# A row-sum kernel: the program's last wait is moved from SyncE to GpSimd

## The chip, the cores and the metric

The kernel runs on one core of a Trainium2 chip. The core has five engines with an instruction stream each: TensorE, VectorE (called DVE in the profile), ScalarE (ACT), GpSimd (POOL) and SyncE (SP). They meet through numbered semaphores alone. The time is that of the device in microseconds (us), from run to run; the profile shows one execution of the program, and its span runs from the program's first instruction to its last.

## The reference

```python
def setup_inputs():
    batch, seq, dim = 32, 512, 1024
    return {"x": np.random.randn(batch, seq, dim).astype(np.float32)}

def reference(x):
    return np.sum(x, axis=-1).astype(np.float32)
```

16,384 rows of 1,024 numbers in float32 are each summed: 67.11 MB are read and 0.07 MB written.

## The kernel before

The rows are laid over 128 partitions, 128 rows to each, in three blocks of 32, 48 and 48 (`BLOCKS`). Each block is cut into groups of 16 rows per partition (`G`), eight groups in all, and three buffers `xt` take them in turn. All transfers, loads and stores, are issued by SyncE, in the order of the list `loads` (L149); a load into a buffer that is in use waits until DVE has done with it. The first row of the first group has a load of its own, so that DVE can start early, and the last group comes in pieces: rows 0 to 8, 9 to 12 and 13 to 14 (`CUTS`), and then the last row in two parts, into the tile `tail`.

DVE sums most rows (L63), and by pairs the row before the end and the last one (L81). ScalarE takes seven rows of the second last group and about half of the last group's first pieces (L74). Sums are collected in `res`. GpSimd has no work in the kernel; it sets four constants at the program's start and takes part in the barriers there (L208, L169).

When the last group's pieces have arrived, SyncE issues three early stores (L155), for all results that are already there; they count up the semaphores `early0` to `early2`. When DVE and ScalarE have done their last instruction, it issues the last store (L159), of the last group's 16 results per partition, which counts up the semaphore `store` by 16 when it has landed. Then the program ends with three steps on SyncE: it waits for the three early stores (L161, recorded on L162), clears all semaphores of the kernel but `store` (L163), and waits for the last store and takes `store` back to zero (L164). The semaphores have to be zero again when the program ends, as the next execution starts from them.

Two of the loads are moved by hand ahead of the starting barrier (`EARLY`), which is why SyncE's first issue opens the span.

Of the kernel before, what the change touches and what calls it, by code (L numbers as in the profile page):

```python
# [19 lines left out]
def row_sums(nc, x: bass.AP, out: bass.AP):  # L20
# [33 lines left out]
    sems = {n: nc.alloc_semaphore(n) for n in names}  # L54
# [106 lines left out]
    for k in range(len(stores)):  # L161
        nc.sync.wait_ge(sems[f"early{k}"], 16)  # L162
    nc.sync.sem_clear(range(numbers[0], sems["store"].num))  # L163
    nc.sync.wait_ge(sems["store"], 16).then_inc(sems["store"], -16)  # L164


def kernel(tc: tile.TileContext, x: bass.AP, out: bass.AP):
    tc.close()
    tc.compile()  # L169
    nc = tc.nc  # L170
    row_sums(nc, x, out)

    sp = mybir.EngineType.SP
    fn = nc.m.functions[0]
    entry, body = None, None
    for blk in fn.blocks:
        ops = [i for i in blk.instructions if i.engine == sp]
        if entry is None:  # L180
            entry = blk
        elif any(i.opcode == "DMACopy" for i in ops):
            body = blk
            break
    code = list(body.instructions)
    loads = [i for i in code if i.engine == sp and i.opcode == "DMACopy"][:EARLY]
    for load in loads:
        assert not load.sync_info.on_wait
        code.remove(load)
    body.instructions = code  # L190
    code = list(entry.instructions)
    at = next(k for k, i in enumerate(code) if i.engine == sp and i.opcode == "Drain")
    code[at:at] = loads
    entry.instructions = code
# [29 lines left out]
```

## Time and profile before

| what | us |
|---|---|
| median of 3 runs | 160.84 |
| the three runs | 160.83, 160.84, 161.23 |
| the profiled execution, its time | 160.73 |
| the profiled execution, its span | 159.4 |
| last store, from issue (157.95) to landing | 1.4 |

The span is shorter than the time, as it holds the program's own instructions alone: what the system runs ahead of them and behind them is outside of it. In the profile, a row such as "L164 SPq EVENT_SEMAPHORE" gives a line of the kernel, the engine whose instruction queue it is (SPq is SyncE's, POOLq GpSimd's), the kind, and then the shortest, median and longest duration in ns and the start of the first and last. The duration of a semaphore instruction begins when what it waits for is there; the wait itself stands in the list of waits. In that list a line gives who waited for whom, the sum in us, how often, and the longest.

Beside instructions, the trace has a record of every change of a semaphore, with its number and time. The kernel's own semaphores have the numbers 99 to 113 (`store` is 113); the starting barriers use 96 and 97. Times of such records are given here in us from the start of the span.

### The profile page before, as it was taken

Reading aid. Unit: us, or ns where it says so; the run is one execution under the profiler, and the core shown is the slowest. Engines: PE = TensorE matmul, PEld = TensorE weight load, DVE = VectorE, ACT = ScalarE, POOL = GpSimd, SP = SyncE. Lnnn points to the kernel's source line nnn. Section 1 sums busy time; section 2 is a strip of 40 time slices with the busy share of each in tenths; the row PEclk is TensorE's granted clock in tenths of the full one; section 3 lists DMA queues with packets and bytes.
Section 4 is the critical chain, followed back from the end, with each engine's and each line's share of the span. In section 5 each row is a group of like instructions: output and inputs, shape, how many; then the busy total and the mean of one; then the engine's idle time right before and its main releaser. Section 6 shows DMA issues by size and latency. Waiting matters only on the chain.

```text
span 159.4 us, 110 instructions
## 1 busy us (share of the span) xinstructions
DVE 121.5 (76%) x17; ACT 17.2 (11%) x31; POOL 0.2 (0%) x4
## 2 busy tenths in 40 slices
DVE  1100059994799968999499994999949999499685
ACT  3000000000000000000000000000000000494694
POOL 0000000000000000000000000000000000000000
DMA  9988996996997989969969969969979799699994
GB/s 378 493 370 370 493 526 263 526 526 263 526 477 312 526 378 411 526 263 526 526 263 526 526 263 526 526 263 526 460 329 526 312 477 526 296 444 444 387 400 151
DMA packets 2448, 67.18 MB, mean 421 GB/s; under 512 B 784, under 2 KB 912, under 8 KB 1168
## 3 DMA queue, kind: packets, MB, share of 16 engines
q1 hardware_dynamic: 2448, 67.18, 98.2%
HBM read 67.11 MB, written 0.07 MB: 421 GB/s over the span
## 4 chain that ended last, share of the span: by engine, by line
DMA 75%; DVE 22%; SPq 1%; issue 0%
DMA xt<-in_x_dram 50%; DMA tail<-in_x_dram 25%; DVE res L63 22%; SPq L149 1%; DVE pairs L81 0%; DVE res L81 0%
## 5 line engine op out<-in xcount | busy, mean ns | idle before, releaser
L63 DVE TENSOR_REDUCE res<-xt 128x16 f32<-128x16384 f32 (+5 forms) x10 | 119.9, 11994 | 34.1 <-DMA xt<-in_x_dram 34.1
L74 ACT ACTIVATE xt<-xt 128x1024 f32<-128x1024 f32 x15 | 15.6, 1043 | 138.3 <-DMA xt<-in_x_dram 138.3
L74 ACT ACTIVATION_READ_ACCUMULATOR xt<-xt 128x1 f32 x15 | 2.8, 187 | 0.0
L107 DVE MEMSET tail<- 128x1 f32 x1 | 0.1, 59 | 2.0 <-PEq L169 2.0
L74 ACT ACT_TABLE_LOAD x1 | 1.3, 1283 | 1.9 <-PEq L169 1.9
L81 DVE CUSTOM_DVE_ANT_0 pairs<-tail 128x272 f32<-128x272 f32 (+1 forms) x2 | 0.9, 428 | 0.1
L81 DVE CUSTOM_DVE_ANT_0 pairs<-xt 128x512 f32<-128x512 f32 x1 | 0.7, 693 | 0.2 <-DMA xt<-in_x_dram 0.2
L81 DVE DVE_READ_ACCUMULATOR2_ANT res<- 128x1 f32 x2 | 0.2, 82 | 0.0
L208 POOL MEMSET const-bfloat16-1.0<- 128x1 bf16 x1 | 0.1, 102 | 0.0
L208 POOL MEMSET const-uint8-127<- 128x1 uint8 x1 | 0.1, 101 | 0.0
L208 POOL MEMSET const-float32-0.0<- 128x1 f32 x1 | 0.1, 99 | 0.2 <-issue 0.2
L208 POOL MEMSET const-float32-1.0<- 128x1 f32 x1 | 0.1, 98 | 0.0
L81 DVE DVE_READ_ACCUMULATOR2_ANT tail<- 128x1 f32 x1 | 0.1, 82 | 0.0
## 6 DMA issues: line engine op xcount, KB each, us to landing
xt<-in_x_dram SPq DMA_DIRECT2D x1, 7680.0 KB, 21.2
xt<-in_x_dram SPq DMA_DIRECT2D x1, 4608.0 KB, 32.6
xt<-in_x_dram SPq DMA_DIRECT2D x1, 2048.0 KB, 37.0
xt<-in_x_dram SPq DMA_DIRECT2D x1, 1024.0 KB, 39.0
xt<-in_x_dram SPq DMA_DIRECT2D x1, 512.0 KB, 3.5
tail<-in_x_dram SPq DMA_DIRECT2D x1, 272.0 KB, 39.2
tail<-in_x_dram SPq DMA_DIRECT2D x1, 240.0 KB, 39.3
xt<-in_x_dram SPq DMA_DIRECT2D x6, 40.8
```

The source lines that it names most:

```text
L63: nc.vector.tensor_reduce(out=res[:, c : c + n], in_=t[:, j * D : (j + n) * D].rearrange("p (j d) -> p j d", d=D), axis=X, op=ADD,).then_i ...
L74: nc.scalar.activation(out=v, in_=v, func=COPY, accum_out=res[:, c + i : c + i + 1]).then_inc(act, 1)
L81: nc.vector.tensor_tensor_reduce(out=pairs[:, 0 : h - a], in0=t[:, a:h], in1=t[:, h:b], scale=1.0, scalar=0.0, op0=ADD, op1=ADD, accum_out ...
L107: nc.vector.memset(tail[:, CUT + 15 : CUT + 16], 0.0).then_inc(vec, 1)
L149: nc.sync.dma_start(out=dst, in_=src).then_inc(s, 16)
L208: nc = _bacc.Bacc("TRN2", target_bir_lowering=False, num_devices=1)
```

## The change

One word on the program's last line: the wait for `store`, and the decrement that goes with it, are given to GpSimd's instruction stream. SyncE's program ends with the clear of the other semaphores.

```diff
     for k in range(len(stores)):
         nc.sync.wait_ge(sems[f"early{k}"], 16)
     nc.sync.sem_clear(range(numbers[0], sems["store"].num))
-    nc.sync.wait_ge(sems["store"], 16).then_inc(sems["store"], -16)
+    nc.gpsimd.wait_ge(sems["store"], 16).then_inc(sems["store"], -16)
```

All other instructions stand on the same engines in the same order.

## The prediction

> **What bounds the kernel now.** I read the page's head and chain first, then SyncE's waits in the last ten microseconds, then the rows of the lines that end the program, and last the semaphore records of the trace. The page first:
>
> ```profile
> span 159.4 us, 110 instructions
> DVE 121.5 (76%) x17; ACT 17.2 (11%) x31; POOL 0.2 (0%) x4
> ...
> q1 hardware_dynamic: 2448, 67.18, 98.2%
> ...
> DMA 75%; DVE 22%; SPq 1%; issue 0%
> ```
>
> The DMA queue is busy for 98.2% of the span, so the body is bound by reading 67.11 MB, and GpSimd does 0.2 us of work in all. Nothing in the body touches the edited line: what counts is what comes after the last data. The chain of waits ends there:
>
> ```profile
> 118.14 39.32 DMA tail<-in_x_dram
> 157.46 0.05 issue
> 157.51 0.41 DVE pairs L81
> 157.92 0.01 DVE res L81
> ```
>
> After 157.93 us only SyncE is at work. Its issues in the timeline, its waits from 150 us on, and the rows of L163 and L164:
>
> ```profile
> 156.22 1.30 SPq L155 DMA_DIRECT2D out_dram<-res  x3
> 157.95 0.33 SPq L159 DMA_DIRECT2D out_dram<-res  x1
> ```
>
> ```profile
> SPq L164 <- SPq L164: 0.6, 1, 0.6
> SPq L162 <- DMA out_dram<-res: 0.4, 1, 0.4
> ```
>
> ```profile
> L163 SPq EVENT_SEMAPHORE_RANGE_CLEAR  x1: 51/51/51, 158.7 to 158.7; - x1
> ```
>
> ```profile
> L164 SPq EVENT_SEMAPHORE  x1: 17/17/17, 159.4 to 159.4; - x1
> ```
>
> The last store is issued at 157.953 us and its sixteenth landing is recorded at 159.361. SyncE has waited for the early stores by 158.660, cleared the other semaphores from 158.729 to 158.780, and then sat 0.6 us in the wait of L164, which starts at 159.378 and ends at 159.395. That is the end of the span.
>
> The profiled execution took 160.73 us against a span of 159.40, so 1.33 us lie around the program. Part of that can be seen in the semaphore records. Semaphore 2, which no line of the kernel uses, is counted up in rounds of nine, once before the program (-0.375 to -0.004 us) and twice after. The round at the end has its updates at 2.127, 157.489, 157.527, 158.076, 159.539, 159.582, 159.620, 159.654 and 159.701 us. Four of the first five follow the end of an engine's work: TensorE's (its barrier row of L169 ends at 1.893 us), ScalarE's (157.376), DVE's (157.925), SyncE's (159.395). That leaves the third, 38 ns behind ScalarE's, for GpSimd. I read it as a chain TensorE, ScalarE, GpSimd, DVE, SyncE and back; the records name no engine, so the order is inferred. After 159.701 the remaining semaphores are written to (until 160.265), and a last round ends at 160.847. So SyncE's end at 159.395 pushes all this, and whoever ends last sets it.
>
> **The change, part by part.** Removed: one wait on SyncE, 17 ns of execution and a 17 ns reaction (159.361 to 159.378). SyncE then ends with its clear at 158.780, 0.615 us earlier. Its four stores and their issues stay where they are, and so do all loads, so the landing at 159.361 stays.
>
> Added: one wait on GpSimd. It stands at the end of GpSimd's program: no instruction of the kernel is behind it, no engine waits for one, and no transfer of GpSimd's queue exists. All that is behind it is GpSimd's place in the chain on semaphore 2. GpSimd sits in it from about 1.9 us to the landing, which costs nothing (ScalarE sits 134.7 us in a wait likewise). Its price has rows:
>
> ```profile
> L169 POOLq EVENT_SEMAPHORE  x4: 17/17/17, 1.4 to 1.8; - x4
> L169 POOLq DRAIN  x2: 34/38/41, 1.2 to 1.5; - x2
> ```
>
> GpSimd's semaphore instruction takes 17 ns like SyncE's. Its reaction is 25 ns: in two of the program's starting barriers the last arrival is recorded at 1.358 and 1.685 us and GpSimd's wait begins at 1.382 and 1.710. So GpSimd ends at 159.361 + 0.025 + 0.017 = 159.403, 8 ns after SyncE in the kernel before. The span becomes 159.40 again.
>
> [...]
>
> Next, GpSimd's step from its last instruction to its update of semaphore 2. No row shows this for GpSimd, because it was always waiting for its predecessor. The others: ScalarE 113 ns (157.376 to 157.489), SyncE 144 (159.395 to 159.539), DVE 151 (157.925 to 158.076), TensorE 234 (1.893 to 2.127). Bounds 113 and 234; I take SyncE's 144, since both end in the same instruction with the same 17 ns.
>
> Then the rest of the chain. When SyncE came last, four updates remained: 159.539 to 159.701, 162 ns. When GpSimd comes last, six remain: GpSimd to DVE to SyncE and all the way back. The records hold a round in which the third came last, before the program: -2.709, -2.665, -2.641, -2.528, -2.490, -2.455, -2.405, which is 304 ns. The round from -0.375 gives 298 for the same stretch. From below, if SyncE's turn took 43 ns as at 159.582 rather than 113: about 230 ns. From above, if GpSimd is not third but first, with 322 ns from its last row (1.805) to 2.127 and a whole round of 371 ns behind it.
>
> Sum: 159.403 + 0.144 + 0.304 = 159.851 in place of 159.701, that is +0.150 us. Low end: 159.403 + 0.113 + 0.230 = 159.746, +0.045. High end: 159.403 + 0.322 + 0.371 = 160.096, +0.395. A gain is excluded inside this reading, since GpSimd's landing, reaction and chain each are no shorter than SyncE's but for the 31 ns between ScalarE's step and SyncE's.
>
> What is late next: the writes to the semaphores and the last round, which begin behind 159.701 and move with it. Against the profiled execution this is 160.73 + 0.15 = 160.88; the median of the three runs, 160.84, lies 0.11 above that execution, so I forecast 160.99, rounded to 161.0. The body cannot hide any of it, nor add to it.
>
> **The rivals.** A difference of under 0.3%, 0.48 us, is what a measurement of this kernel hardly tells from none; the three runs alone span 0.40 us.
>
> Slower: GpSimd has work of its own behind the program, before it enters the chain. In the kernel before this would have been hidden, because GpSimd is done at 1.8 us and is called at 157.5. In the long round before the program GpSimd's place (-2.709) came 627 ns behind ScalarE's (-3.336), where the other hops are 24 to 50 ns and one 113, so something there kept it back. Its drains of 34 to 41 ns, against 7 to 10 of the others, point the same way, but weakly. Against it: its share of the semaphore writes (numbers 105 to 155, 159.760 to 160.060) is as quick as its neighbours'. If 627 ns come on top of the 144, the end is 159.403 + 0.771 + 0.304 = 160.478, +0.78, and the time 161.62. It decides from the point where GpSimd's step is longer than 144 + 330 = 474 ns, which is where the whole loss passes 0.48 us.
>
> Faster: the time is closed by SyncE's own stream, or by what it does for the queue that it alone issues on, and not by the last engine. SyncE ends 0.615 us earlier, so 160.84 - 0.62 = 160.22. Against it: its semaphore writes (numbers from 207 on) start at 159.664, behind the chain's turn, so SyncE cannot run ahead of the others.
>
> No change at all: what follows the span is not in the time, or is of fixed length. Then only the 8 ns count, 160.85. For it: I do not see where the 160.73 begin and end. Against it: 1.33 us more than the span must come from somewhere, and the records hold 1.45 us behind it.
>
> That the change does not do what it says I can leave aside: the wait stands at the end of GpSimd's program, and the landings it waits for are the same sixteen.
>
> **How the numbers follow.** The forecast 0.56; GpSimd's own work 0.30; no change at all 0.06; SyncE closes the time 0.08. The forecast has more than half because each of its terms has a row, and the second has 0.30 because the one step without a row is the one that it speaks of. Faster by over 0.3% is the last, 0.08; within 0.3% the first and third, 0.62; slower 0.30. The range is 160.7 to 161.65: from a little under no change, for the scatter of the runs, up to the slower rival's 161.62; it leaves out the faster one's 0.08 and some scatter. The forecast's own range is 160.84 + 0.045 to 160.84 + 0.395, 160.89 to 161.24.
>
> By Runtime: NRT & Kernel Launch of the Trainium skill (section The ~15µs preamble/postamble breakdown) a hop of such a barrier over five engines takes 44 ns, eight in all. Six hops would be 264 ns where the rows have 304, and the sum 160.95; the measured round decides.
>
> **What would show it.** The span of the changed kernel should be 159.4, with SyncE's last row the clear of L163 and a GpSimd row of 17 ns on L164 some 25 ns behind the last landing. On semaphore 2, the third update should stand some 0.14 us behind that row, and six more should follow within 0.30 us, so that the round ends about 0.49 us behind the landing's last record instead of 0.34. A third update over 0.47 us behind the GpSimd row proves the slower rival; a round that ends by itself as before, with a shorter time, the faster one. I am wrong too if the landing itself moves, since I left the body untouched.

## The result and the profile after

| | before | after |
|---|---|---|
| median of 8 runs, us | 160.74 | 161.31 |
| the runs, us | 160.62 to 161.23 | 161.01 to 161.61 |
| profiled execution, time, us | 160.73 | 161.42 |
| profiled execution, span, us | 159.4 | 159.5 |

The ratio is 1.0032, with a 95% interval from 1.0022 to 1.0042: about half a microsecond lost. Run again later, the changed kernel gave 1.0035 (1.0021 to 1.0050). The page of the changed kernel, its head, its queue and its chain:

```profile
span 159.5 us, 110 instructions
...
DVE 121.5 (76%) x17; ACT 17.2 (11%) x31; POOL 0.2 (0%) x4
...
q1 hardware_dynamic: 2448, 67.18, 98.0%
...
DMA 75%; DVE 22%; SPq 1%; issue 0%
```

The body is as it was. SyncE's waits from 150 us on, and the rows of L163 and L164 after the change:

```profile
SPq L159 <- DVE res L81: 0.4, 1, 0.4
SPq L162 <- DMA out_dram<-res: 0.4, 1, 0.4
```

```profile
L163 SPq EVENT_SEMAPHORE_RANGE_CLEAR  x1: 51/51/51, 158.9 to 158.9; - x1
```

```profile
L164 POOLq EVENT_SEMAPHORE  x1: 17/17/17, 159.5 to 159.5; - x1
```

SyncE no longer waits for the last store, its program ends with the clear of L163, and the wait of L164 is GpSimd's, of the same 17 ns. In the span, then, next to nothing is lost (8 ns, as the table shows). The loss lies behind it, in the records of semaphore 2. The table has the end of both profiled executions, in us, and in ns the parts in between:

```
                                        before      after
last landing of the store              159.361    159.496
the last engine's program ends         159.395    159.538     34 ->  42
its update of semaphore 2              159.539    160.099    144 -> 561
last update of that round              159.701    160.383    162 -> 284
last update of the last round          160.847    161.531   1146 -> 1148
landing to end of the first round                            340 -> 887
```

Read from the top: the landing itself came 135 ns later in this execution. The last store was issued that much later already, at 158.09 us in place of 157.95, because the loads ended later:

```profile
158.09 0.33 SPq L159 DMA_DIRECT2D out_dram<-res  x1
```

This is scatter of the loads, not the edit: a second execution of the changed kernel has the landing at 159.450 us, and two of the kernels below with the last wait on SyncE have it at 159.205 and 159.521. From the landing to the end of the round it is 547 ns more: 8 for the reaction, 417 more in the step from the last engine's last instruction to its update, 122 for the rest of the chain. What follows is the same length. 135 + 547 + 2 make 0.684 us, and the two profiled times differ by 0.69.

### The profile page after: what moved, and what is told of

Its sections match the earlier page's. It is cut to its first block, busy times and chain, and to the rows that moved or that the text cites. A ratio compares the mean times of both kernels' runs of the same rounds, so it can differ in the third digit from the quotient of the medians.

```text
span 159.5 us, 110 instructions
## 1 busy us (share of the span) xinstructions
DVE 121.5 (76%) x17; ACT 17.2 (11%) x31; POOL 0.2 (0%) x4
## 4 chain that ended last, share of the span: by engine, by line
DMA 75%; DVE 22%; SPq 1%; issue 0%
DMA xt<-in_x_dram 50%; DMA tail<-in_x_dram 25%; DVE res L63 22%; SPq L149 1%; DVE pairs L81 0%; DVE res L81 0%
```

## Experiments

**GpSimd ends early, SyncE keeps the last wait** (`gp_early`). The first early store's semaphore is moved behind those of the other two in the list of names (the first two lines of the edit), so that SyncE's clear stops ahead of it.

```diff
-    names += ["tail1", "vec", "act", "early0", "early1", "early2", "store"]
+    names += ["tail1", "vec", "act", "early1", "early2", "early0", "store"]
     ...
-    for k in range(len(stores)):
+    for k in (1, 2):
         nc.sync.wait_ge(sems[f"early{k}"], 16)
-    nc.sync.sem_clear(range(numbers[0], sems["store"].num))
+    nc.sync.sem_clear(range(numbers[0], sems["early0"].num))
+    nc.gpsimd.wait_ge(sems["early0"], 16).then_inc(sems["early0"], -16)
     nc.sync.wait_ge(sems["store"], 16).then_inc(sems["store"], -16)
```

> SyncE keeps the last wait; GpSimd waits for the first early store instead and takes its semaphore back. Theory A (GpSimd has a step of its own of about 0.56 us between its last instruction and its update of semaphore 2, whatever it waited for): GpSimd ends about 157.7 us, its update follows about 0.56 us later, near 158.25, where it stood at 157.53 before; SyncE's update at about 159.54 still comes later, so the time is that of before, 160.74 within 0.1%. Theory B (the step is that dear only for the engine that ends last, for instance because the others are already waiting): the update stands about 0.15 us behind GpSimd's last instruction, time 160.74 as well.

Measured: 0.9991 (0.9978 to 1.0004). GpSimd's row, in the view of its line:

```profile
L164 POOLq EVENT_SEMAPHORE  x1: 17/17/17, 157.9 to 157.9; - x1
```

It ends at 157.896, and the third update of semaphore 2 comes at 158.457: 561 ns, to the nanosecond the step of the changed kernel, though SyncE's program ends 1.66 us later (159.555). From the last landing (159.521) to the end of the round it is 340 ns, as in the kernel before. So the step does not come from ending last; it is there all the time, and in the kernel before it was hidden, because GpSimd had nothing to do from 1.8 us on. Theory B falls.

**The last wait on each of the other engines** (`last_act`, `last_dve`, `last_pe`). One word is changed on the last line, here for ScalarE:

```diff
-    nc.sync.wait_ge(sems["store"], 16).then_inc(sems["store"], -16)
+    nc.scalar.wait_ge(sems["store"], 16).then_inc(sems["store"], -16)
```

> ScalarE holds the last wait. Theory A (the loss belongs to GpSimd): reaction 22 ns, 17 ns, step 113 ns, then 336 ns of chain: 0.49 us from the last landing record to the end of the round in place of 0.34, so +0.15 us, ratio 1.001. Theory C (any engine other than SyncE pays about 0.42 us more than its hops): 0.90 us, +0.57 us, ratio 1.0035.

> VectorE holds the last wait. Theory A: reaction 28 ns, 21 ns, step 151 ns, then 254 ns of chain: 0.45 us from the last landing record to the end of the round, +0.11 us, ratio 1.0007. Theory C: 0.87 us, +0.53 us, ratio 1.0033.

> TensorE, which heads the chain, holds the last wait. Theory A: reaction 30 ns, 51 ns, step 234 ns, then the whole round of 371 ns: 0.69 us from the last landing record to the end of the round, +0.35 us, ratio 1.002. Theory C: 1.1 us, +0.77 us, ratio 1.0048.

Measured: 1.0015 (1.0006 to 1.0024), 1.0012 (1.0003 to 1.0021) and 1.0026 (1.0013 to 1.0039). The rows of the last line, first the kernel with ScalarE, then with VectorE, then with TensorE:

```profile
L164 ACTq EVENT_SEMAPHORE  x1: 17/17/17, 159.4 to 159.4; - x1
```

```profile
L164 DVEq EVENT_SEMAPHORE  x1: 21/21/21, 159.3 to 159.3; - x1
```

```profile
L164 PEldq EVENT_SEMAPHORE  x1: 51/51/51, 159.2 to 159.2; - x1
```

From the records, in ns (the sum of a row is the way from the last landing to the end of the round):

```
last engine   landing to its end   step   rest of the chain    sum
TensorE               79            279          357           715
ScalarE               38            149          324           511
GpSimd                42            561          284           887
VectorE               49            182          240           471
SyncE                 34            144          162           340
```

The rest of the chain falls from row to row by 33 to 78 ns. That shows the order, which the prediction had only inferred: TensorE, ScalarE, GpSimd, VectorE, SyncE, and back. The records show it directly too: with the wait on TensorE no update stands ahead of the wait's end, with ScalarE one, GpSimd two, VectorE three and SyncE four, and the others follow one after another. The steps of TensorE, ScalarE and VectorE are 31 to 45 ns longer here than the 234, 113 and 151 ns in the prediction, where another instruction was their last; so a step is not one number for an engine. All three results lie by theory A (0.51, 0.47 and 0.71 us where 0.49, 0.45 and 0.69 were expected) and far from theory C. GpSimd is the only engine with a step over 0.3 us, so its loss is more than its place in the chain.

**More instructions on GpSimd behind the wait** (`gp_pad`).

```diff
-    nc.gpsimd.wait_ge(sems["store"], 16).then_inc(sems["store"], -16)
+    nc.gpsimd.wait_ge(sems["store"], 16).then_inc(sems["store"], 1)
+    for i in range(17, 24):
+        nc.gpsimd.wait_ge(sems["store"], i).then_inc(sems["store"], 1)
+    nc.gpsimd.wait_ge(sems["store"], 24).then_inc(sems["store"], -24)
```

> As the changed kernel, but the wait is followed on GpSimd by eight more semaphore instructions that have nothing to wait for (about 78 ns each by the starting barriers, some 0.62 us in all). Theory A (fixed work behind the program's end): the step from GpSimd's last instruction to its update of semaphore 2 stays 0.56 us, and the time grows by the eight instructions, to about 161.9, ratio to before 1.007. Theory D (the step is code or a state that is fetched once GpSimd wakes, and that goes on beside whatever it executes): the eight instructions hide most of it, the step falls below 0.3 us, and the time is about that of the changed kernel, ratio 1.003.

Measured: 1.0069 (1.0050 to 1.0088). The added seven in the middle, in the view of their line:

```profile
L166 POOLq EVENT_SEMAPHORE  x7: 17/17/17, 159.5 to 160.0; - x7
```

They follow each other in 96 ns. The expected 78 ns are from a starting barrier, where the second instruction waits for nothing; here, by the edit, each waits for the update of the one before. GpSimd's program ends at 160.139, the update comes at 160.700: 561 ns again. From the landing to the end of the round it is 1.653 us, 0.766 more than in the changed kernel, which is eight times 96 ns to within 2 ns. Nothing of the step is hidden by instructions ahead of it. Theory D falls.

**Work for GpSimd's processors behind the wait** (`gp_memset`).

```diff
     nc.gpsimd.wait_ge(sems["store"], 16).then_inc(sems["store"], -16)
+    nc.gpsimd.memset(pairs[0][:, 0:1], 0.0)
```

> As the changed kernel, with one memset of a column on GpSimd behind the wait, so that its processors have just worked when the program ends. Theory A: step of about 0.56 us behind the memset's end, time 0.1 to 0.3 us over that of the changed kernel, ratio 1.004 to 1.005. Theory E (the step is the answer of processors that have been idle for 157 us): it falls by 0.2 us or more, and the time is no longer than that of the changed kernel.

Measured: 1.0039 (1.0019 to 1.0059), which does not tell it from the changed kernel. The records do:

```profile
L165 POOL MEMSET pairs<- x1: 99/99/99, 160.0 to 160.0; 128x1 f32 x1
```

The wait ends at 159.883, the memset runs from 159.985 to 160.084, and the update comes at 160.596: 512 ns behind the memset, 713 behind the wait, which is 561 + 152. Counted from the memset's end the step is 49 ns shorter, not 0.2 us, so theory E falls. What the 49 ns are is open: they may run beside the memset, or depend on which instruction is the last, as the three engines above also had steps 31 to 45 ns shorter behind another one.

**GpSimd ends a little before SyncE** (`gp_thr`).

```diff
-    for k in range(len(stores)):
+    for k in (0, 1):
         nc.sync.wait_ge(sems[f"early{k}"], 16)
-    nc.sync.sem_clear(range(numbers[0], sems["store"].num))
+    nc.sync.sem_clear(range(numbers[0], sems["early2"].num))
+    for i in range(16, 22):
+        nc.gpsimd.wait_ge(sems["early2"], i).then_inc(sems["early2"], 1)
+    nc.gpsimd.wait_ge(sems["early2"], 22).then_inc(sems["early2"], -22)
     nc.sync.wait_ge(sems["store"], 16).then_inc(sems["store"], -16)
```

> SyncE keeps the last wait. GpSimd waits for the third early store (landing some 0.72 us before the last) and then has six semaphore instructions more, so that it ends about 0.2 us before the last landing. Theory A with a step of 561 ns and 284 ns of chain behind it: GpSimd's update comes about 0.35 us behind the last landing and, although SyncE's program is the last to end, GpSimd ends the round, about 0.64 us behind the landing: +0.30 us, ratio 1.002. Theory B (only the engine whose program ends last pays): ratio 1.000, the round 0.34 us behind the landing.

Measured: 1.0016 (0.9997 to 1.0036), medians 161.10 and 160.75: by the times alone unclear. GpSimd's six rows ahead of its last, and SyncE's last row:

```profile
L165 POOLq EVENT_SEMAPHORE  x6: 17/17/17, 158.7 to 159.1; - x6
```

```profile
L167 SPq EVENT_SEMAPHORE  x1: 17/17/17, 159.3 to 159.3; - x1
```

GpSimd's program ends at 159.258, SyncE's at 159.364. Yet the third update of semaphore 2 comes at 159.819 (561 ns behind GpSimd's end), the fifth, SyncE's, only at 159.887, and the round ends at 160.105, 0.775 us behind the last landing (159.330). Expected were 0.64; the six instructions took 96 ns each in place of 78, which makes 0.11 us of the difference, and the third early store landed 0.69 us ahead of the last in place of 0.72, which makes the rest. Here GpSimd decides although it ends first, so theory B falls here too. From the table above a break-even can be estimated: GpSimd has to be done 561 + 284 - 340 = 505 ns before the last landing to cost nothing. Here it was done 72 ns before, and the round ended 435 ns later than 340 ns behind the landing, 2 ns from what the estimate gives; an end near the break-even itself was not run.

**GpSimd's program without its first instructions** (`gp_bare`), and the changed kernel once more (`after_again`).

```diff
+    pool = mybir.EngineType.Pool
+    code = [i for i in code if not (i.engine == pool and i.opcode in ("ISA", "Memset"))]
     entry.instructions = code
```

> As the changed kernel, but GpSimd's instructions at the program's start, INC_SWDGE_SEM and the four memsets of constants that no instruction of this kernel reads, are taken out, so that GpSimd has nothing but barriers and the last wait. Theory A (fixed work behind the program, whatever the program did): step 561 ns, time that of the changed kernel, ratio 1.003. Theory F (the step closes something that the program opened on GpSimd, its processors or its queue): the step falls towards the 144 to 182 ns of SyncE, ScalarE and VectorE, and the ratio towards 1.0009.

> The changed kernel once more. Theory A: step 561 ns and 284 ns of chain to within some ns, ratio within 1.0022 to 1.0042. Theory G (the step varies from execution to execution, as the landing of the last store does): another step, by 50 ns or more.

Measured: `after_again` 1.0035 (1.0021 to 1.0050), step 160.052 - 159.491 = 561 ns, chain 285. Theory G falls: the landing scatters, the step does not. `gp_bare` has the same step (160.166 - 159.605) and 284 ns of chain, so theory F falls as well. But its ratio is 0.9926 (0.9911 to 0.9941), which no theory had: 159.74 us for a profiled execution whose span is 159.6 us and whose last round ends at 161.599. By the records it does nothing faster.

**Where the time begins** (`sp_nomemset`). In the other profiled executions the time is shorter than the end of the last round by 0.11 to 0.12 us, in `gp_bare` by 1.86. Something that was taken out had started the count. The last kernel leaves the wait on SyncE and takes out the memsets on GpSimd alone:

```diff
+    pool = mybir.EngineType.Pool
+    code = [i for i in code if not (i.engine == pool and i.opcode == "Memset")]
     entry.instructions = code
```

> The kernel before, with the last wait on SyncE, and only the four memsets of unread constants at GpSimd's program start taken out; INC_SWDGE_SEM stays. Theory H (the time is counted from the first memset or other compute instruction, 0.23 us before, which then is VectorE's memset at 1.98 us): the span and the records of the end stay, the round still ends 0.34 us behind the last landing, and the time falls by 1.75 us to about 158.95, ratio 0.989, without any work being done sooner. Theory I (it is counted from GpSimd's first row, INC_SWDGE_SEM at 0.13 us): no change, ratio 1.000.

Measured: 0.9899 (0.9883 to 0.9916), 158.99 us. The program's start in the timeline of the kernel before, and then of this one:

```profile
0.00 2.71 SPq L149 DMA_DIRECT2D xt<-in_x_dram  x4
0.23 0.10 POOL L208 MEMSET const-float32-0.0<- 128x1 f32 x1 [0.23 <-issue]
...
1.91 1.28 ACT L74 ACT_TABLE_LOAD   x1 [1.91 <-PEq L169]
1.98 0.06 DVE L107 MEMSET tail<- 128x1 f32 x1 [1.98 <-PEq L169]
```

```profile
0.00 2.72 SPq L149 DMA_DIRECT2D xt<-in_x_dram  x4
1.92 1.28 ACT L74 ACT_TABLE_LOAD   x1 [1.92 <-PEq L169]
1.99 0.06 DVE L107 MEMSET tail<- 128x1 f32 x1 [1.99 <-PEq L169]
```

The loads are issued and the table is loaded at the same places; only GpSimd's rows are gone. The span is 159.2 us and the end of the first round lies 340 ns behind the last landing (159.205 to 159.545), as before. The distance from the end of the last round to the time, in which the scatter of the landing falls out, shows where the count begins: it grows by 1.763 us from the kernel before to this one, and by 1.748 from the changed kernel to `gp_bare`. The first memsets lie 1.758 (0.231 to 1.989) and 1.750 us (0.230 to 1.980) apart. ScalarE's table load stands ahead of VectorE's memset, at 1.921 and 1.910 us, but would make only 1.690 and 1.680. So the count moves with the first memset, and begins neither with SyncE's issue at 0.00, nor with INC_SWDGE_SEM, nor with the table load. Whether any other compute instruction would start it as well was not tried. It is the fastest kernel here by the metric, and not by the work: the results reach memory no sooner.

## Why the prediction was right in its range and wrong in its likeliest case

- *The range and the forecast*: the median of 161.31 lies inside the range of 160.7 to 161.65, but above the forecast's own 160.89 to 161.24. The difference says it better, as the forecast stood on the 160.84 of three runs and the median of eight is 160.74: +0.57 us by the medians and +0.547 by the records, above the forecast's highest +0.395 and below the slower rival's +0.78. The range held because it was drawn up to the slower rival, which had a chance of 0.30.
- *The wait itself*: right. 25 ns of reaction and 17 ns were forecast and measured; the span, forecast as 159.40, was 159.54 with a landing 0.135 us later.
- *SyncE's earlier end gains nothing*: right. After the change SyncE's update follows VectorE's in 24 ns (160.142 to 160.166), so it stood ready and waited. SyncE ending the time by itself is refuted: its stream ended 0.6 us ahead and the time grew.
- *The order of the chain*: inferred in the prediction, shown by the three kernels with another last engine. The rest behind GpSimd was sized 304 ns from a round before the program and measured 284, the difference being mostly SyncE's turn (97 ns against 113). The 44 ns a hop of Runtime: NRT & Kernel Launch in the Trainium skill (The ~15µs preamble/postamble breakdown) agree with a whole round as a mean (357 ns over eight hops with TensorE last), not hop by hop: these took 23 to 97 ns there.
- *What follows moves with it*: right, 1146 and 1148 ns, and with it the rival in which the end is not in the time falls.
- *The step that failed*: "GpSimd's step from its last instruction to its update of semaphore 2". The prediction took SyncE's 144 ns, since both end in the same instruction, and bounds of 113 and 234 from the other engines' rows; it is 561 ns. With it in the sum, the forecast +0.150 us becomes +0.567, and with the chain's 284 ns the measured +0.547. Four engines' rows are no bounds for a fifth whose step had always been hidden, and the high end of 322 ns, for another order of the chain, was none either.
- *The slower rival*: its mechanism is what happened. It put GpSimd's step at 144 + 627 = 771 ns and its point of decision at 474; the step was 561. The 627 ns that it was sized by are no measure: the same distance in the long round before the program was 1249 ns in the changed kernel's profile and 967 in that of `gp_bare`. Nor was GpSimd's place the one slow place there: ScalarE's (-3.336) came 4.937 us behind TensorE's (-8.273), a hop that the prediction passed over when it gave the others as 24 to 50 ns and one 113. (This long round also makes two rounds before the program, not one.) That the rival's number came near is luck, and since the range's upper end is that number, it is in part luck too that the range held.
- *The bound of 0.3%*: the loss, 0.32%, lies at it, with an interval to both sides. What tells it from none is the records, where scatter of the landing falls out.

What GpSimd does in its 561 ns stays open. It is time that passes behind the program's last instruction, it is the same 561 ns in six executions and 49 ns less behind the memset, and it does not depend on when GpSimd ends, on the semaphore instructions just before, or on the memsets and the INC_SWDGE_SEM at its program's start; the trace has no rows of it.

## What to carry to other kernels

The engine whose program ends late pays its own way out of the program, and these ways differ: before the last wait is moved, look in the records of the closing round at what each engine has behind its last instruction, and treat an engine that has always been early as unknown. SyncE, which with the last wait on it had both the shortest step (144 ns) and the shortest rest of the chain (162 ns), was the right place for that wait here; GpSimd, by the estimate above, had to be done half a microsecond before the last landing to be free. Where a time moves without the span and the records, ask first where the count begins.

## What had not been expected of the hardware

GpSimd's step out of the program is exact behind a semaphore wait: 561 ns each time, where 144 to 279 ns were measured for the others with the last wait on them, while the landing of the last store scattered by over 0.6 us between profiled executions (159.189 to 159.842). And the measured time moved with the first memset, whether it was GpSimd's or VectorE's, and not with the first transfer: with that memset 1.76 us later the median fell by 1.68 us (160.67 to 158.99).
